# Memory keys and values projected two heads at a time, the filters' skip row added by a product with ones, and the decay gates' exponentials taken over four heads at once

## The chip, the cores and the metric

The kernel runs on one core of one Trainium2 chip. The metric is the device time of one execution in microseconds (us). A core has TensorE (PE in the rows, with its weight loads as PEld), VectorE (DVE), ScalarE (ACT), GpSimd (POOL) and SyncE (SP), whose queue issues the DMAs. Each engine works through its own list of instructions in order; an instruction that waits holds up everything behind it on its engine.

## What is computed

The reference is a trunk of two encoder layers on 512 tokens of width 1024, in fp32. Each layer runs three mixers side by side (attention with two key/value heads, a Hyena long convolution, gated linear attention), merges them with gates, then a cross-attention of four heads 256 wide into a memory of 256 tokens, then an MLP of width 4096. Three pieces of it matter here:

```
# cross-attention: keys and values of the memory, 4 heads of 256
k = rmsnorm((mn @ wk).reshape(B, M, X_HEADS, X_HEAD_DIM), kn)
v = (mn @ wv).reshape(B, M, X_HEADS, X_HEAD_DIM)
# Hyena: filters of order 2, normalised by their column sums of |f|, and a skip
f = f / (jnp.sum(jnp.abs(f), axis=0, keepdims=True) + EPS)
y = irfft(rfft(u, 2L) * rfft(f)) + u * skip
# gated linear attention: decay gates of 4 heads, two directions
g = jax.nn.log_sigmoid(lr @ w_lr + b_lr) / 16
b = jnp.cumsum(g, over a chunk of 64 tokens)      # then exp(b), exp(-b)
```

## The kernel before

Every fp32 product is made of three matmuls: `split` writes a rounded high part (a cast on ACT, `wh` or `xh`) and the rest (a subtraction on DVE, `wl` or `xl`), and `mm3` (L245 to L249) adds hi·hi, hi·lo and lo·hi into one PSUM tile. Weights come as chunks of 128 x 1024: a DMA into one of two `wr` buffers, a cast into one of three `wh`, a subtraction into one of three `wl`. A chunk of a token projection feeds 24 matmuls of 128x512.

The work of a layer is cut into generators (stages), and an order written out by hand (`ORDER0` for layer 0, `ORDER` for layer 1) says which stage emits its next piece. `kv` is the memory's keys and values, `mx` the norm of the layer's input, `gp` and `ga0` the linear attention's projections and gates, `fi` the Hyena filters, `at` the attention, `gh` the Hyena projection. A scheduler with priorities (`late`, `AHEAD`, `SPLIT_AHEAD`) makes each engine's list from that. The filters of layer 1 are made while PE runs the MLP of layer 0.

**Memory.** The stage works one head at a time, four values (V0 to V3), then four keys (K0 to K3). A head takes two chunks (4 k-tiles of 256 columns each), and its two token halves are two runs of `proj_tm` into one PSUM tile of 128 x 2 x 256: 24 matmuls of 128x256 for each half, 48 for a head and 384 for a layer. The stage keeps two PSUM tiles. A value is copied out by ACT. A key is squared by ACT (L1192), scaled by a reciprocal root of small DVE instructions (L347 to L352), multiplied by DVE (L1197), transposed and stored.

**Norm.** `mx` waits for a sum of squares `hsum` (L328), which PE adds over partitions (L336) and, after a reciprocal root, spreads over them (L358). DVE then multiplies eight tiles (`nrm`, L384) and makes their low parts (`xl`, L243), in part with POOL. The first product of the layer's input that follows is the gates' low-rank projection (L886, L888), which needs all eight `xl`.

**Filters.** A filter block (eight in all, four for each layer) has `acc`, the sums of absolute values by partition. PE adds them over partitions into a row of 1x256 with ones as the weights (L706, fp32), DVE multiplies the row by the skip weights on one partition (L712), and PE spreads the row over 128 partitions into the tile `T4[0]` with a row of ones (L718, fp32). A second product of `acc` (L708) gives the column sums as a column for the normaliser.

**Gates.** For each head PE makes the logits (L922), ACT takes Abs (L925), Exp (L928) and Ln (L933) in tiles of 128x512, POOL subtracts (L940), DVE scans forward and backward (L941, L943), POOL copies chunk ends (L955, L956), DVE shifts (L950), ACT takes the two exponentials (L952, L953), DVE multiplies queries and keys (L959, L960). Exp and Ln lie in different function tables of ACT, so a switch between them is an ACT_TABLE_LOAD. The gate `gt` of L1072 is a further exponential.

## Time and profile before

| | before |
|---|---|
| runs, us | 2300.2, 2301.21, 2303.95 (median 2301.21) |
| profiled execution, us | 2299.69 |
| its span from the first to the last instruction, us | 2297.8 |
| mean granted TensorE clock | 0.985 |
| PE busy | 2211.1 us, 96% of the span, 11432 instructions |
| DVE, ACT, POOL busy | 67%, 44%, 18% |

The profiled execution is 2299.69 us long; 1.9 us of it lie outside the span. Its busy time of PE counts an instruction from its start to its modelled end, and matmuls overlap, so what a matmul costs in a stream is read from start to start. A granted clock of 1.00 in a stretch means 2.4 GHz; half of it is 1.2 GHz.

### The profile page before, as it was taken

Reading aid. Unit: us, or ns where it says so; the run is one execution under the profiler, and the core shown is the slowest. Engines: PE = TensorE matmul, PEld = TensorE weight load, DVE = VectorE, ACT = ScalarE, POOL = GpSimd, SP = SyncE. Lnnn points to the kernel's source line nnn. Section 1 sums busy time; section 2 is a strip of 40 time slices with the busy share of each in tenths; the row PEclk is TensorE's granted clock in tenths of the full one; section 3 lists DMA queues with packets and bytes.
Section 4 is the critical chain, followed back from the end, with each engine's and each line's share of the span. In section 5 each row is a group of like instructions: output and inputs, shape, how many; then the busy total and the mean of one; then the engine's idle time right before and its main releaser. Section 6 shows DMA issues by size and latency. Waiting matters only on the chain.

```text
span 2297.8 us, 29857 instructions
## 1 busy us (share of the span) xinstructions
PE 2211.1 (96%) x11432; PEld 1857.2 (81%) x11432; DVE 1535.5 (67%) x2491; ACT 1013.0 (44%) x1635; POOL 418.1 (18%) x353
## 2 busy tenths in 40 slices
PE   6989999998899999999999989999989999999999
PEld 6877888887678878888887978888867788888887
DVE  7799856869665755766476786667886566444445
ACT  5667744323344544443336577443323444433231
POOL 1141101224220101111051130012253101000004
PEclk9999999999999999999999999999999999999999
DMA  6423123123143133332244321242222422323222
GB/s 224 146 97 106 65 74 123 56 93 101 60 149 113 63 122 103 122 122 101 92 143 143 105 79 41 74 128 65 83 101 74 141 89 74 101 92 101 94 94 97
DMA packets 78966, 232.58 MB, mean 101 GB/s; under 512 B 9054, under 2 KB 10086, under 8 KB 78824
## 3 DMA queue, kind: packets, MB, share of 16 engines
q1 hardware_dynamic: 75656, 224.91, 29.7%
q0 software_dynamic: 3168, 5.77, 0.9%
q8 instruction: 90, 1.47, 0.3%
q14 instruction: 52, 0.43, 0.1%
HBM read 213.87 MB, written 16.78 MB: 100 GB/s over the span
## 4 chain that ended last, share of the span: by engine, by line
PE 78%; DVE 13%; ACT 3%; DMA 2%; issue 2%; POOL 1%; SPq 0%; DVEq 0%; ACTq 0%; POOLq 0%
PE ps L249 24%; PE ps L247 24%; PE ps L248 24%; DVE wl L232 3%; PE ps L533 1%; ACT wh L231 1%; DVE ts L796 1%; PE ps L520 1%; PE ps L542 1%; PE ps L544 1%; DMA wr<-in_x_wv_dram 1%; PE ps L521 1%; DMA F<-F 1%; DVE u L797 1%; DVE ts L587 1%
## 5 line engine op out<-in xcount | busy, mean ns | idle before, releaser
L232 DVE TENSOR_TENSOR wl<-wr,wh 128x1024 fp32r<-128x1024 f32 x340 | 432.7, 1275 | 257.6 <-ACT wh L231 253.1
L231 ACT CAST wh<-wr 128x1024 fp32r<-128x1024 f32 x344 | 357.9, 1042 | 554.1 <-PE ps L248 459.8
L249 PE MATMUL ps<-xh,wl 128*128 128x512 f32 x1344 | 532.8, 397 | 17.2 <-DVE wl L232 17.2
L247 PE MATMUL ps<-xh,wh 128*128 128x512 f32 x1344 | 534.3, 398 | 2.3 <-ACT wh L231 2.0
L248 PE MATMUL ps<-xl,wh 128*128 128x512 f32 x1344 | 532.3, 396 | 0.0
L249 PEld LDWEIGHTS ps<-xh,wl 128*128 128x128 f32 x1344 | 255.4, 190 | 72.6 <-DVE wl L232 20.9
L247 PEld LDWEIGHTS ps<-xh,wh 128*128 128x128 f32 x1344 | 255.6, 190 | 55.7 <-ACT wh L231 3.3
L248 PEld LDWEIGHTS ps<-xl,wh 128*128 128x128 f32 x1344 | 255.6, 190 | 50.4
L249 PE MATMUL ps<-hdh,wl 128*128 128x512 f32 x512 | 199.9, 390 | 0.0
L247 PE MATMUL ps<-hdh,wh 128*128 128x512 f32 x512 | 199.7, 390 | 0.0
L248 PE MATMUL ps<-hdl,wh 128*128 128x512 f32 x512 | 199.2, 389 | 0.0
L1344 DVE TENSOR_TENSOR macc<-ps,macc 128x512 f32<-128x512 f32 x96 | 66.1, 689 | 86.0 <-PE ps L249 86.0
L249 PEld LDWEIGHTS ps<-hdh,wl 128*128 128x128 f32 x512 | 96.1, 188 | 22.1 <-issue 2.3
L248 PEld LDWEIGHTS ps<-hdl,wh 128*128 128x128 f32 x512 | 96.1, 188 | 19.9
L247 PEld LDWEIGHTS ps<-hdh,wh 128*128 128x128 f32 x512 | 96.1, 188 | 19.9 <-issue 0.3
L1346 POOL TENSOR_TENSOR macc<-macc,rb 128x512 f32<-128x512 f32 x16 | 23.6, 1472 | 398.4 <-DVE macc L1344 398.4
L248 PE MATMUL ps<-wl,xh 128*128 128x256 f32 x320 | 91.5, 286 | 0.8 <-DVE wl L232 0.8
L247 PE MATMUL ps<-wh,xh 128*128 128x256 f32 x320 | 91.4, 286 | 0.1
L249 PE MATMUL ps<-wh,xl 128*128 128x256 f32 x320 | 91.3, 285 | 0.0
L248 PE MATMUL ps<-wl,mnh 128*128 128x256 f32 x256 | 77.0, 301 | 13.9 <-DVE wl L232 13.8
L1328 DVE TENSOR_TENSOR rl<-rl 128x512 f32<-128x512 f32 x64 | 44.7, 699 | 65.9 <-ACT rl L1327 65.9
L247 PE MATMUL ps<-wh,mnh 128*128 128x256 f32 x256 | 76.2, 298 | 7.8 <-ACT wh L231 7.8
(404 smaller groups left out, 4570.8 us busy)
## 6 DMA issues: line engine op xcount, KB each, us to landing
wr<-in_mlp_w_dram SPq DMA_DIRECT2D x128, 512.0 KB, 3.5
wr<-in_w_in_dram SPq DMA_DIRECT2D x108, 512.0 KB, 3.6
wr<-in_x_wv_dram SPq DMA_DIRECT2D x16, 512.0 KB, 3.6
wr<-in_x_wk_dram SPq DMA_DIRECT2D x16, 512.0 KB, 4.0
F<-ff SPq DMA_DIRECT2D x32, 256.0 KB, 2.3
F<-F SPq DMA_DIRECT2D x32, 256.0 KB, 5.2
wr<-in_w_out_dram SPq DMA_DIRECT2D x16, 512.0 KB
wr<-in_x_wq_dram SPq DMA_DIRECT2D x16, 512.0 KB, 3.6
```

The lines of the kernel that those rows point to most:

```text
L231: r = self.nc.scalar.copy(hi, src)
L232: (lo_eng or self.nc.vector).tensor_tensor(lo, src, hi, op=ALU.subtract)
L247: mm(out, lh, rh, start=start, stop=False, skip_group_check=True)
L248: mm(out, lh, rl, start=False, stop=False, skip_group_check=True)
L249: mm(out, ll, rh, start=False, stop=stop, skip_group_check=True)
L520: nc.tensor.matmul(s, QH[:, tk], K2, start=True, stop=False)
L521: nc.tensor.matmul(s, QL[:, tk], K2, start=False, stop=True)
L533: nc.tensor.transpose(pt[:, k, i * P:(i + 1) * P], Pn[i][:, (2 * kp + k) * P:(2 * kp + k + 1) * P], self.ident)
L542: nc.tensor.matmul(ov, vv, TH[:, k], start=(kt == 0), stop=False, skip_group_check=True)
L1328: nc.vector.tensor_tensor(r, r, r, op=ALU.mult)
L1344: nc.vector.tensor_tensor(acc[m], ps, acc[m], op=ALU.add)
L1346: nc.gpsimd.tensor_tensor(acc[m], acc[m], rb, op=ALU.mult)
```

## The change

It has four parts.

Keys and values go two heads at a time (`proj_mem`): the weights are laid out on the host as chunks of 2 k-tiles of 512 columns, and each chunk is used for both token halves before the next. The moving operand is 512 wide, the two PSUM tiles hold one token half each, and a layer has 192 matmuls of 128x512 for 384 of 128x256. A pair has four copies or squares into the tiles of its two heads, and one reciprocal root for both keys.

The skip row is multiplied before it is summed: DVE multiplies all 128 partitions of `acc` (with EPS/128 added) by skip weights that the host has repeated on 128 partitions, splits the product, and two fp32r matmuls with a matrix of ones add it over partitions and spread it at once into `T4[0]`. The products L706 and L718 go, L708 (L741 after) stays. The ones are a tile of their own.

The four heads' gates share one tile `ab` of 128 x 4 x 512: four Abs, one Exp and one Ln over 2048 columns.

The order lists lose the `kv` pieces that are merged. K0 stood ahead of `mx` in both; now V01 and V23 stand ahead of it and K01 behind three pieces of `gp`.

```
-ORDER0: kv kv kv lx kv kv kv mx fi gp gp kv gp fi at at at gp at fi ... fi kv at kv ga0 at ...
+ORDER0: kv kv lx kv mx fi gp gp kv gp fi at at at gp at fi ... fi kv at ga0 at ...
-ORDER:  kv kv kv kv kv kv mx gp gp gp kv at at at at ga0 kv gp at ... gh gh gh kv gh ...
+ORDER:  kv kv kv mx gp gp gp kv at at at at ga0 gp at ... gh gh gh kv gh ...

+    def proj_mem(self, W, hp, X):
+        ps = [self.ps("mm") for _ in range(2)]
+        for g in range(4):
+            raw = self.wbuf("wr")
+            self.last_w = self.nc.sync.dma_start(raw, W[hp, g])
+            ...
+                self.split(raw, hi, lo)
+            for mt in range(2):
+                tk = slice(mt * P, (mt + 1) * P)
+                for k in range(2):
+                    kt = 2 * g + k
+                    self.mm3(ps[mt], X[kt][0][..., tk], X[kt][1][..., tk], hi[:, k], lo[:, k], kt == 0, kt == 7)
+        return ps

-                    nc.tensor.matmul(ps[0:1, 0:256], self.ones[:, 0:1], acc, start=True, stop=True)
...
-                row = self.rowbuf
-                self.load(row, I["hy_skip"][l, o, c])
-                nc.vector.scalar_tensor_tensor(row, ps[0:1, 0:256], EPS, row, op0=ALU.add, op1=ALU.mult)
-                with self.late("fr"):
-                    nc.tensor.matmul(T4[0][:, 0], self.ones[0:1, :], row, start=False, stop=True,
+                sa = self.t("F", (P, 2, 256), F32, "skip")[:, 0]
+                nc.vector.scalar_tensor_tensor(sa, acc, EPS / P, skip, op0=ALU.add, op1=ALU.mult)
+                sb = self.t("F", (P, 2, 256), F32R, "skip2")
+                self.split(sa, sb[:, 0], sb[:, 1])
+                with self.late("fr"):
+                    for x in range(2):
+                        nc.tensor.matmul(T4[0][:, 0], self.ones_r, sb[:, x], start=False, stop=(x == 1),

+        xs = self.t("ab4", (P, 4, L), F32, "ab")
         for h in range(4):
...
-            nc.scalar.activation(c, ps, AF.Abs, bias=b)
+            nc.scalar.activation(xs[:, h], ps, AF.Abs, bias=b)
...
-            nc.scalar.activation(c, c, AF.Exp, scale=-1.0)
-        for c in xs:
-            nc.scalar.activation(c, c, AF.Ln, bias=self.ones[:, 0:1])
+        nc.scalar.activation(xs, xs, AF.Exp, scale=-1.0)
+        yield
+        nc.scalar.activation(xs, xs, AF.Ln, bias=self.ones[:, 0:1])

-        for h in range(4):
-            w = self.wchunk(I["x_wk"][l], h)
+        for hp in range(2):
+            ps = self.proj_mem(I["x_wk"][l], hp, X)
...
-            self.rsqrt(rk, ss)
+            rk = self.tiny(4, "krs")
+            self.rsqrt(rk, ss)
```

Three places show how the instructions move. The line numbers of the changed kernel are its own.

PE at the start of layer 1, before: the last product of layer 0 (`hdh`), the sum of squares of the memory (L1160), the first matmuls of the memory's values (`mnh`, `mnl`), and, 120 of them later, the norm's sum over partitions (L336).

```order
L249 MATMUL ps_10226<-hdh_9945,wl_75 128x512
L1160 MATMUL ps_10287<-consts,memsq_10246 128x1 x4
L247 MATMUL ps_10312<-wh_71,mnh_10248 128x256
...
L248 MATMUL ps_10430<-wl_74,mnh_10281 128x256
L249 MATMUL ps_10430<-wh_70,mnl_10282 128x256
L336 MATMUL ps_10625<-consts,hsum_10107 128x1
L247 MATMUL ps_10430<-wh_72,mnh_10248 128x256
L336 MATMUL ps_10625<-consts,hsum_10107 128x1 x3
```

The same place in the changed kernel: L1184 is the memory's sum, L251 to L253 are `mm3`, L359 is the norm's sum and L381 its spread.

```order
L253 MATMUL ps_10028<-hdh_9747,wl_75 128x512
L1184 MATMUL ps_10089<-ones,memsq_10048 128x1 x4
L251 MATMUL ps_10108<-wh_72,mnh_10050 128x512
...
L253 MATMUL ps_10108<-wh_73,mnl_10062 128x512
L359 MATMUL ps_10248<-ones,hsum_9909 128x1 x4
L251 MATMUL ps_10108<-wh_73,mnh_10061 128x512
...
L253 MATMUL ps_10108<-wh_71,mnl_10073 128x512
L381 MATMUL ps_10265<-consts,small 128x128 x4
L251 MATMUL ps_10109<-wh_71,mnh_10072 128x512
```

The norm's sum stood behind 120 matmuls of the memory and now stands behind 15, with 81 of V01 and V23 behind it; K01 is no longer ahead of the norm at all.

ACT in the gates of layer 1, before: Exp (L928) and Ln (L933) of the third and fourth head, each with its table load, casts of weights (L231, `wh`) and the exponential of the gate (L1072, `gt`).

```order
L928 ACTIVATE ab_11605<-ab_11605 128x512
L925 ACTIVATE ab_11612<-ps_11610,consts 128x512
L933 ACT_TABLE_LOAD
L933 ACTIVATE ab_11605<-ab_11605,consts 128x512
L928 ACT_TABLE_LOAD
L928 ACTIVATE ab_11612<-ab_11612 128x512
L1072 ACTIVATE gt_11785<-ps_11760 128x512
L933 ACT_TABLE_LOAD
L933 ACTIVATE ab_11612<-ab_11612,consts 128x512
L231 CAST wh_72<-wr_69 128x1024
L952 ACT_TABLE_LOAD
L952 ACTIVATE mn_11593<-ab_11591 128x512
```

The same in the changed kernel, from the third head's Abs (L951) on: Exp is L955, Ln L957, the cast L235, the gate L1096.

```order
L951 ACTIVATE ab_11156<-ps_11167,consts 128x512
L951 ACTIVATE ab_11156<-ps_11172,consts 128x512
L955 ACTIVATE ab_11156<-ab_11156 128x2048
L1096 ACTIVATE gt_11346<-ps_11321 128x512
L957 ACT_TABLE_LOAD
L957 ACTIVATE ab_11156<-ab_11156,ones 128x2048
L235 CAST wh_71<-wr_70 128x1024
L235 CAST wh_72<-wr_69 128x1024
L1096 ACT_TABLE_LOAD
L1096 ACTIVATE gt_11373<-ps_11348 128x512
L976 ACTIVATE mn_11160<-ab_11156 128x512
```

All four heads' Ln stand in one instruction, and two casts of weights wait behind it.

DVE in the same gates, before: the scans (L941, L943), the reciprocal root of K2 (L350 to L352) and the two low parts of weights (L232) behind the fourth head's first scan.

```order
L941 SCALAR_TENSOR_TENSOR ab_11598<-reset_12221,mn_11600 64x512
L352 SCALAR_TENSOR_TENSOR small<-small 128x2
L950 TENSOR_TENSOR ab_11591<-ab_11591,small 128x512
L1197 SCALAR_TENSOR_TENSOR xk_11564<-ps_11515,small,xgain_10542 128x256 x2
L943 SCALAR_TENSOR_TENSOR ab_11598<-reset_12221,mn_11600 64x512
L941 SCALAR_TENSOR_TENSOR ab_11605<-reset_12221,mn_11607 64x512
L950 TENSOR_TENSOR ab_11598<-ab_11598,small 128x512
L943 SCALAR_TENSOR_TENSOR ab_11605<-reset_12221,mn_11607 64x512
L941 SCALAR_TENSOR_TENSOR ab_11612<-reset_12221,mn_11614 64x512
L232 TENSOR_TENSOR wl_74<-wr_69,wh_72 128x1024
L232 TENSOR_TENSOR wl_75<-wr_68,wh_70 128x1024
```

And after: L965 and L967 are the scans, L974 the shift, L236 the low parts of weights, L983 and L984 the products with queries and keys.

```order
L953 TENSOR_SCALAR mn_11175<-ps_11172,consts 128x512
L965 SCALAR_TENSOR_TENSOR ab_11156<-reset_11779,mn_11160 64x512
L236 TENSOR_TENSOR wl_76<-wr_70,wh_71 128x1024
L236 TENSOR_TENSOR wl_74<-wr_69,wh_72 128x1024
L967 SCALAR_TENSOR_TENSOR ab_11156<-reset_11779,mn_11160 64x512
L965 SCALAR_TENSOR_TENSOR ab_11156<-reset_11779,mn_11165 64x512
L974 TENSOR_TENSOR ab_11156<-ab_11156,small 128x512
L967 SCALAR_TENSOR_TENSOR ab_11156<-reset_11779,mn_11165 64x512
L965 SCALAR_TENSOR_TENSOR ab_11156<-reset_11779,mn_11170 64x512
L983 SCALAR_TENSOR_TENSOR qk_1677_10397<-qk_1677_10397,mn_11160 128x512
L984 TENSOR_TENSOR qk_1683_10465<-qk_1683_10465,ab_11156 128x512
```

The pair of low parts stood behind seven scans; now it stands behind the first alone, and the next one (`wl_75`) twelve instructions further on. The reciprocal root and the two products of K2 are gone from here.

## Rows read from the trace of the kernel before

**Rows 1.** The page: busy time, share of the span and instructions of each engine; the chain that ended last, by engine.
```profile
PE 2211.1 (96%) x11432; PEld 1857.2 (81%) x11432; DVE 1535.5 (67%) x2491; ACT 1013.0 (44%) x1635; POOL 418.1 (18%) x353
PE 78%; DVE 13%; ACT 3%; DMA 2%; issue 2%; POOL 1%; SPq 0%; DVEq 0%; ACTq 0%; POOLq 0%
```

**Rows 2.** The two longest sums in the waits of PE (waiting line, what it waited for: us in total, times, the longest).
```profile
PE ps L249 <- DVE wl L232: 31.4, 16, 5.2
PE ps L248 <- DVE wl L232: 14.6, 9, 5.9
```

**Rows 3.** Windows of 20 us: busy time and instructions of PE, PEld, DVE, ACT, POOL, then the granted clock of TensorE, the DMA share and GB/s.
```profile
40.00:60.00 20.00, 18.64 (x111) 15.85 (x112) 15.50 (x30) 9.48 (x18) 0.82 (x2) 0.85 0.63 190
140.00:160.00 20.00, 16.69 (x65) 12.94 (x66) 19.44 (x35) 16.04 (x22) 9.13 (x13) 0.74 0.26 80
1040.00:1060.00 20.00, 20.00 (x107) 17.15 (x106) 11.83 (x19) 10.43 (x16) 3.92 (x3) 1.00 0.16 54
1320.00:1340.00 20.00, 14.75 (x63) 11.84 (x63) 19.14 (x30) 14.85 (x24) 10.12 (x10) 0.90 0.21 69
```

**Rows 4.** The timeline of PE (start, duration, line, operation, tiles; idle time before and its releaser): nine steps of memory matmuls in a stream, then the wait of layer 0's start, and the first and last matmul at a low clock behind it (24 steps apart).
```profile
33.01 0.28 PE L247 MATMUL ps<-wh,mnh 128*128 128x256 f32 x1
34.09 0.28 PE L247 MATMUL ps<-wh,mnh 128*128 128x256 f32 x1
40.29 0.58 PE L248 MATMUL ps<-wl,mnh 128*128 128x256 f32 x1 [5.92 <-DVE wl L232]
40.67 0.41 PE L249 MATMUL ps<-wh,mnl 128*128 128x256 f32 x1
45.79 0.32 PE L249 MATMUL ps<-wh,mnl 128*128 128x256 f32 x1
```

**Rows 5.** The timeline of PE in the MLP of layer 0: two matmuls of 128x512 in a stream, 25 steps apart.
```profile
1100.13 0.39 PE L247 MATMUL ps<-xh,wh 128*128 128x512 f32 x1
1105.80 0.39 PE L248 MATMUL ps<-xl,wh 128*128 128x512 f32 x1
```

**Rows 6.** The timeline of PE in the MLP of layer 0, around the filter products of one block.
```profile
1061.78 0.39 PE L249 MATMUL ps<-xh,wl 128*128 128x512 f32 x1
1062.10 0.59 PE L706 MATMUL ps<-acc,consts 128*1 128x256 f32 x2
1062.62 0.61 PE L708 MATMUL ps<-consts,acc 128*128 128x1 f32 x4
1063.97 0.69 PE L718 MATMUL ps<-consts 1*128 1x256 f32 x2
1064.60 0.50 PE L247 MATMUL ps<-hdh,wh 128*128 128x512 f32 x1
```

**Rows 7.** The timelines of DVE, ACT and PE at the norm of layer 0: the first `nrm`, the wait of a cast for a key chunk, the low part that waited for the cast, the last `xl`, and the last instruction of the low-rank projection.
```profile
31.68 4.08 DVE L384 TENSOR_TENSOR nrm<-rb,h 128x512 f32<-128x512 f32 x3 [1.42 <-ACT rb L378]
47.71 1.05 ACT L231 CAST wh<-wr 128x1024 fp32r<-128x1024 f32 x1 [6.57 <-DMA wr<-in_x_wk_dram]
48.79 1.23 DVE L232 TENSOR_TENSOR wl<-wr,wh 128x1024 fp32r<-128x1024 f32 x1 [3.77 <-ACT wh L231]
51.73 0.74 DVE L243 SCALAR_TENSOR_TENSOR xl<-nrm,consts,xh 128x512 fp32r<-128x512 f32 x1
60.43 0.39 PE L888 MATMUL ps<-xl,wh 128*32 128x512 f32 x1
```

**Rows 8.** The timelines of PE and DVE at the start of layer 1: the sum of squares on DVE, the norm's sum on PE, PE's longest wait, the last `xl`, the low-rank projection's last instruction.
```profile
1198.48 0.68 DVE L328 TENSOR_TENSOR hsum<-hsum,hsq 128x512 f32<-128x512 f32 x1
1209.94 0.28 PE L336 MATMUL ps<-consts,hsum 128*128 128x1 f32 x2
1227.12 0.58 PE L248 MATMUL ps<-wl,mnh 128*128 128x256 f32 x1 [3.67 <-DVE wl L232]
1231.49 0.75 DVE L243 SCALAR_TENSOR_TENSOR xl<-nrm,consts,xh 128x512 fp32r<-128x512 f32 x1 [0.34 <-ACT xh L242]
1236.26 0.39 PE L888 MATMUL ps<-xl,wh 128*32 128x512 f32 x1
```

**Rows 9.** The timelines of ACT and PE in the gates of layer 0: a wait of ACT ahead of the first exponential with a cast behind it, and PE's wait for that cast.
```profile
142.38 0.63 ACT L952 ACTIVATE mn<-ab 128x512 f32<-128x512 f32 x1 [2.11 <-DVE ab L950]
142.92 1.03 ACT L231 CAST wh<-wr 128x1024 fp32r<-128x1024 f32 x1
144.00 0.80 PE L247 MATMUL ps<-xh,wh 128*128 128x512 f32 x1 [1.65 <-ACT wh L231]
```

**Rows 10.** The timelines of ACT, DVE and PE in the gates of layer 1: a table load and the Exp behind it, a scan, the pair of low parts of weights behind the scans, and the two waits of PE there.
```profile
1325.00 1.28 ACT L928 ACT_TABLE_LOAD   x1
1326.30 0.63 ACT L928 ACTIVATE ab<-ab 128x512 f32<-128x512 f32 x1
1332.16 1.22 DVE L941 TENSOR_TENSOR_SCAN ab<-reset,mn 64x512 f32<-64x512 f32 x1
1337.61 2.35 DVE L232 TENSOR_TENSOR wl<-wr,wh 128x1024 fp32r<-128x1024 f32 x2
1338.87 0.80 PE L249 MATMUL ps<-xh,wl 128*128 128x512 f32 x1 [5.25 <-DVE wl L232]
1352.04 0.30 PE L499 MATMUL ps<-consts,q 128*128 128x128 f32 x1 [1.43 <-ACT gt L1072]
```

**Rows 11.** The instructions on the tile `mn` (line, engine, operation, count: duration in ns, least, median and most; first and last start; forms): POOL's subtraction in the gates.
```profile
L940 POOL TENSOR_TENSOR mn<-mn,ab x8: 1257/1298/1890, 134.8 to 1334.1; 128x512 f32<-128x512 f32 x8
```

More of the change, by code (lines that the diff above doesn't have):

```diff
@@ L108, in laid_out @@
     o["w_glr"] = chunks(w[:, :, 3840:3872], 32)
[L109 to L110 removed]
+    for n in ("w_br_attn", "w_br_hyena", "w_br_gla", "w_out", "x_wq", "x_wo", "mlp_w1", "mlp_w2"):
         o[n] = chunks(a[n])
+    for n in ("x_wk", "x_wv"):
+        d, k, m = a[n].shape
+        o[n] = f(a[n].reshape(d, k // 256, 2, P, m // 512, 512).transpose(0, 4, 1, 3, 2, 5)).reshape(
+            d, m // 512, k // 256, P, 1024)
     col = lambda x: x.reshape(depth, -1, P).transpose(0, 2, 1)
@@ L289, in setup @@
         nc, cp = self.nc, self.cp
-        C = cp.tile([P, 1408], F32, name="consts")
-        self.rowbuf = C[0:1, 1152:1408]
+        C = cp.tile([P, 1280], F32, name="consts")
+        self.skip = C[:, 1024:1280]
+        self.ones_r = cp.tile([P, P], F32R, name="ones")
         self.small = cp.tile([P, 2 * SMALL], F32, name="small")
@@ L295, in setup @@
         self.turn = dict(wr=0, wh=0, wl=0)
-        self.ident, self.ones = C[:, 0:P], C[:, P:2 * P]
+        self.ident, self.ones = C[:, 0:P], self.ones_r.bitcast(F32)
         self.rope = C[:, 256:768].rearrange("p (a t d) -> p a t d", a=2, t=NT)
@@ L660, in filters @@
                 acc = self.t("s12", (P, 2, 256), F32, "acc")[:, 0]
+                skip = self.skip
+                self.load(skip, I["hy_skip"][l, o, c])
                 for par in (1, 0):
@@ L1183, in cross_kv @@
         G = G[:, 0]
-        for h in range(4):
-            w = self.wchunk(I["x_wk"][l], h)
-            ps = self.ps("mm", (P, 2, 256))
-            for mt in range(2):
-                self.proj_tm(ps[:, mt], w, slice(0, 256), X, slice(mt * P, (mt + 1) * P))
-            kk = self.t("st", (P, 2, 256), F32, "xk")
-            ss = self.tiny(2, "kss")
-            for mt in range(2):
-                nc.scalar.activation(kk[:, mt], ps[:, mt], AF.Square, accum_out=ss[:, mt:mt + 1])
-            nc.vector.scalar_tensor_tensor(ss, ss, 1.0 / 256, me, op0=ALU.mult, op1=ALU.add)
-            rk = self.tiny(2, "krs")
-            self.rsqrt(rk, ss)
-            for mt in range(2):
-                nc.vector.scalar_tensor_tensor(kk[:, mt], ps[:, mt], rk[:, mt:mt + 1], G,
-                                               op0=ALU.mult, op1=ALU.mult)
-            pt = self.ps("b", (P, 2, 256))
-            for dt in range(2):
-                for mt in range(2):
-                    with self.late("kt"):
-                        nc.tensor.transpose(pt[:, dt, mt * P:(mt + 1) * P],
-                                            kk[:, mt, dt * P:(dt + 1) * P], self.ident)
-            xk = self.t("xk", (P, 2, 256), F32, "xk")
-            nc.scalar.copy(xk, pt)
-            nc.sync.dma_start(self.kvd[h].rearrange("p (a b) -> p a b", a=2), xk)
@@ new lines, in cross_kv @@
+        for hp in range(2):
+            ps = self.proj_mem(I["x_wk"][l], hp, X)
+            kks = []
+            ss = self.tiny(4, "kss")
+            for j in range(2):
+                kk = self.t("st", (P, 2, 256), F32, "xk")
+                for mt in range(2):
+                    nc.scalar.activation(kk[:, mt], ps[mt][:, 256 * j:256 * j + 256], AF.Square,
+                                         accum_out=ss[:, 2 * j + mt:2 * j + mt + 1])
+                kks.append(kk)
+            for j in range(2):
+                s2 = ss[:, 2 * j:2 * j + 2]
+                nc.vector.scalar_tensor_tensor(s2, s2, 1.0 / 256, me, op0=ALU.mult, op1=ALU.add)
+            rk = self.tiny(4, "krs")
+            self.rsqrt(rk, ss)
+            for j in range(2):
+                kk = kks[j]
+                for mt in range(2):
+                    nc.vector.scalar_tensor_tensor(kk[:, mt], ps[mt][:, 256 * j:256 * j + 256],
+                                                   rk[:, 2 * j + mt:2 * j + mt + 1], G, op0=ALU.mult, op1=ALU.mult)
+            for j in range(2):
+                kk = kks[j]
+                pt = self.ps("b", (P, 2, 256))
+                for dt in range(2):
+                    for mt in range(2):
+                        with self.late("kt"):
+                            nc.tensor.transpose(pt[:, dt, mt * P:(mt + 1) * P],
+                                                kk[:, mt, dt * P:(dt + 1) * P], self.ident)
+                xk = self.t("xk", (P, 2, 256), F32, "xk")
+                nc.scalar.copy(xk, pt)
+                nc.sync.dma_start(self.kvd[2 * hp + j].rearrange("p (a b) -> p a b", a=2), xk)
```

51 lines of the change are left out of this document (24 added, 27 removed).

## The prediction

> **What bounds the kernel now.** The page comes first: PE is busy 96% of the span and the chain that ended last runs 78% through PE [rows 1]. So time is won in two ways only: less work on PE, or less of its waiting. The waits of PE come next: nearly all are for low parts of weights, 46 us in 25 waits [rows 2]; a low part is a DVE instruction, so these are places where DVE is late. The windows show where [rows 3]: at 40 to 60, 140 to 160 and 1320 to 1340 us PE loses both busy time and clock (0.85, 0.74, 0.90), with DVE at 19.1 to 19.4 of 20 in the last two; in the MLP (1040 to 1060) PE is 20.00 of 20 at a clock of 1.00. There every PE step removed is time won; near the two starts and the gates a step removed may only lengthen a wait.
>
> The timeline gives the price of a step, from start to start. Memory matmuls of 128x256: 1.08 us for nine steps, 0.120 each; at the low clock 5.12 us for 24, 0.213 each [rows 4]. Matmuls of 128x512: 5.67 us for 25, 0.227 each [rows 5].
>
> **The change, part by part.** All gains are in us of PE's end.
>
> *Filters in the MLP: +4.0.* Around L706, 0.84 us pass from one `mm3` step to the next product; a plain step is 0.227, so L706's pair costs 0.61. L718's pair takes 0.63 to the next step [rows 6]. Removed 1.24 a block, added two 256-wide fp32r steps at 0.12, net 1.0; four blocks lie here. If the new pair breaks the stream as L706 did, 0.63 a block remains: 2.5. The DVE, ACT work added (a multiplication, a cast, a subtraction of 128x256) lies beside a PE that waits for neither here. Bounds 2.5 to 5.
>
> *Filters of layer 0: +2.0.* The same 4.0, but in a stretch where DVE is as full as PE [rows 3]. Each block has one more DVE instruction (the subtraction) there. I take half; bounds 0 and 4.
>
> *Memory matmuls.* A head costs 48 x 0.120 = 5.76 before and 24 x 0.227 = 5.44 after, so 0.32 a head and 5.1 for all 16. The lower bound is 0 (two half-wide steps as dear as a wide one). The values are inside the two start terms below; the keys of layer 1 stand in stretches bound by PE: +1.3; those of layer 0 in the DVE-bound stretch, half: +0.7.
>
> The Trainium skill (TensorE: Matmul & The Clock Gate, "Wait — 56ns, not 53.3ns?") gives a warm matmul N/2.4 GHz plus about 2.5 ns, which is an estimated 109 and 216 ns here and 0.06 us a head, 1.0 in all. The rows, 120 and 227, differ from it; by the page the whole forecast would be about 1.7 us longer, 2284.
>
> *Start of layer 0: +3.0.* DVE goes from the first `nrm` at 31.68 to the last `xl`, ending at 52.47, in 20.8 us, 3.77 of them idle for the cast of a key chunk, which waited 6.57 for its DMA [rows 7]. K0's chunks are no longer ahead, so that wait goes and the last `xl` ends near 48.7. The low-rank projection is 16 steps of 0.23; it ended at 60.8, now at 48.7 + 3.7 = 52.4: 8.4 earlier. K0's 5.44 is still to be done later, so 3.0 is won. The wait of 5.92 for a low part behind three `nrm` [rows 4] stays in some form: the `nrm` are still ahead of it in DVE's list. If taking K0 out of the gap only lengthens PE's idling, the gain is 0; if K0 later fills a wait, 6.
>
> *Start of layer 1: +4.0.* DVE had the sum of squares at 1199.16, PE added it at 1209.94 only, since 120 memory matmuls stood ahead [rows 8]. With 15 ahead it runs at about 1199.2, 10.7 earlier. If the chain to the last `xl` (end 1232.24) moves with it, that ends at 1221.5, the projection at 1225.3 instead of 1236.65: 11.3 earlier, 5.9 after K0's 5.44 is paid. Off that, two things. V23's first matmul needs a PSUM tile that V01 held (both tiles are one pair's; before, heads alternated): three copies of 256 columns, each about 0.3 to 0.4 by the 1.03 of a 1024-column cast [rows 9], an estimated 1.0. And V23's four low parts fall between the `nrm`, with DVE and POOL both at work: 0.9. The 3.67 wait for a low part [rows 8] does not vanish: PE has 81 matmuls (18.4 us) to cover 22 us of the norm. Bounds 0 and 6.
>
> *Gates of layer 1: +2.6.* Before: waits of 5.25 and 1.43 [rows 10]. After, the first scan needs all four heads. From the second pair of logits: Abs twice 1.3; Exp of 2048 columns; `gt` 0.6; load 1.28; Ln; POOL's subtraction 1.30 [rows 11]; scan 1.22. Exp of 512 is 0.63 [rows 10], a 1024 cast 1.03 [rows 9], so 0.40 per 512 and 1.83 for 2048. Sum 9.4, then a low part of 1.23 [rows 7]: 10.6. Two chunks have their low parts ahead of it in DVE's list, 48 x 0.227 = 10.9 of PE: a wait of 0 to 1.4, say 0.7. The next low part but one stands behind six scans (7.3) and six 128x512 instructions at the 0.75 of an `xl` [rows 8] (4.5); with two low parts that is 14.3 against 10.9 of PE: a wait of 3.4. So 4.1 for 6.7. What leaves this queue is the reciprocal root and products of K2; K2's 5.8 us of matmuls, which covered PE here, leave too, and that is in the count of chunks. Bounds -8 (PE has no chunk ahead) and +8.7 (no wait, and the 2.0 us that a clock of 0.90 costs in 20).
>
> *Gates of layer 0: +1.0.* Now a cast stands behind an exponential that waited 2.11 for DVE, PE waits 1.65 for that cast [rows 9], and the clock of 0.74 costs 5.2 in the window [rows 3]. The four loads fewer per layer are 5.1 us of ACT, but two casts now stand behind load and Ln, 3.1 in a piece. Bounds -8 and +6.9.
>
> Two reciprocal roots fewer in a layer take DVE time off; I count it in the terms above. DMAs keep their number; the eight skip loads carry 128 KB for one row and are needed long after issue.
>
> Sum: 4.0 + 2.0 + 1.3 + 0.7 + 3.0 + 4.0 + 2.6 + 1.0 = 18.6. The profiled execution took 2299.7, of which the span is 2297.8; so 2281.1. It lies 1.5 under the median of the runs, 2301.2, so I forecast 2282 to 2283 and write 2282.
>
> **The rivals.** 0.2% is 4.6 us, about what a measurement of this kernel can tell from no change.
>
> (a) *The gates in one piece starve PE in both layers; slower.* For it: the first scan is one DVE instruction with two low parts queued behind it, and the chain to it is serial. If PE has no chunk ahead, the first wait is 10.6; if the scans also wait for POOL's four subtractions (5.2), the second is 8.6; 24 steps at the low clock lose 2.2. That is 21.4 a layer, 42.8, against 15.6 now (5.25 + 1.43 + 2.0, and 1.65 + 5.2). It costs 27 where the other terms give 15: 2313. It decides from 35 us of such loss, 17.6 a layer. Against it: the casts and low parts of two chunks are ahead in the lists.
>
> (b) *Only arithmetic pays.* At both starts PE idles through the norm as DVE dictates, and removing K0 buys nothing. 4.0 + 2.0 + 5.1 = 11: 2290. For it: DVE at those places makes what PE waits for.
>
> (c) *The waits go too.* ACT and DVE lose loads and reciprocal roots just where they are late; the gates' 15.6, starts of 6 and 6, all 8 of the filters and 2.5 of the keys: 38, so 2263.
>
> (d) *No change.* As (a), but without POOL's part: 16.2 a layer, 32.4 against 15.6, so 17 lost for 15 won: 2303.
>
> (e) *A wide step wins next to nothing over two narrow ones.* If the step is N columns and a small fixed cost, the memory matmuls give 1.7 less and 2284 comes out; the rows at 0.120 and 0.227 speak against it. The page cited above states this rule.
>
> **How the numbers follow.** The forecast as summed (2273 to 2288) 0.53; (e), inside it, 0.05; (b) 0.15; (c) 0.12; (d) 0.08; (a) 0.07. The predicted time is that of the first. Leaving out (a) and (d) leaves 0.85, and the range runs from (c)'s 2264 to 2297, past (b)'s 2290 by the 7 us that the gates can add to it. Faster by over 0.2% holds all but (d) and (a), 0.85; within, 0.08; slower, 0.07.
>
> **What will show it.** In the profile after: memory matmuls of 128x512 at 0.227 a step, 384 of them; in the MLP, a filter block with two steps of 0.12 where 1.24 stood, and PE still 20.00 of 20; the norm's sum on PE within a microsecond of DVE's at layer 1's start, and the low-rank projection's end about 11 before its place then, with one key head more behind it; at layer 0's start no wait of a cast for a key chunk and that projection done near 52; in layer 1's gates a wait under 1.5 before the first low part behind a scan and one of about 3.4 after it. I am wrong if PE idles over 10 us in a gate stage, if PE's gap at the starts grows by what K0 filled, or if the fp32r pair costs as much as the two fp32 products. A wait of PE for a copy of V01 above 1 us would be the PSUM tile mis-sized.

## The result and the profile after

The changed kernel takes 2287.8 us (median of 4 runs, 2285.6 to 2291.0), the kernel before beside it 2300.7: 0.9944 of it, interval 0.9932 to 0.9957. Timed again later beside three experiments it gave 0.9945 (0.9933 to 0.9958). So 13 us are won where 18.6 were forecast: the direction and the range held, and the gain came out a third smaller.

The page after: busy time of each engine, and the chain by engine. They answer to [rows 1].

```profile
PE 2196.0 (96%) x11032; PEld 1827.7 (80%) x11032; DVE 1530.7 (67%) x2455; ACT 1001.3 (44%) x1623; POOL 416.8 (18%) x353
PE 71%; DVE 11%; issue 2%; DMA 2%; ACT 2%; POOL 0%; SPq 0%; DVEq 0%; ACTq 0%; POOLq 0%
```

PE's share is as before: its busy time fell from 2211.1 to 2196.0 us, and the rest of the span did not fall (86.7 before, 88.5 after). Its longest sums of waits after (answer to [rows 2]):

```profile
PE ps L253 <- DVE wl L236: 32.3, 18, 4.6
PE ps L251 <- ACT wh L235: 14.7, 11, 7.5
PE ps L252 <- DVE wl L236: 9.3, 7, 2.8
PE ps L543 <- ACT qh L531: 3.8, 1, 3.8
```

Before, the waits for casts of weights and for `qh` were these:

```profile
PE ps L247 <- ACT wh L231: 12.1, 8, 7.6
PE ps L520 <- ACT qh L508: 0.5, 2, 0.2
```

Low parts still cost 41.6 us in 25 waits for 46.0 in 25, casts of weights cost 14.7 for 12.1, and the wait for `qh` rose from 0.5 to 3.8.

To see where the 13 us lie, the program is cut at PE instructions that both kernels have. The table gives the us that each stretch takes in a profiled execution (the changed kernel twice). Up to some cuts (the ends of A, H, I and J) the changed kernel has one key head still to do that the kernel before has done; "net" is before less after with that head set at 5.44 us.

| stretch, up to | before | after | again | net gain | forecast |
|---|---|---|---|---|---|
| A: layer 0's low-rank projection | 60.4 | 52.7 | 53.2 | +2.3, +1.8 | +3.0 |
| B: the first logits | 66.4 | 69.7 | 70.6 | +2.1, +1.2 | 0 |
| C: the linear attention's norm (337 us) | 210.2 | 211.2 | 213.0 | -1.0, -2.8 | +3.7 |
| D: the cross-attention's norm (692 us) | 355.0 | 357.1 | 357.3 | -2.1, -2.3 | 0 |
| E, F: the first filter block in the MLP | 188.8 | 187.2 | 187.2 | +1.6, +1.6 | 0 |
| G: the end of the MLP | 314.0 | 308.8 | 308.8 | +5.2, +5.2 | +4.0 |
| H: layer 1's low-rank projection | 41.6 | 31.4 | 31.2 | +4.8, +5.0 | +4.0 |
| I: layer 1's last logits | 82.6 | 82.0 | 82.2 | +0.6, +0.4 | +1.3 |
| J: the attention's scores behind the gates | 58.1 | 58.5 | 58.5 | -0.4, -0.4 | +2.6 |
| K: the last norm | 575.5 | 580.6 | 580.3 | +0.3, +0.6 | 0 |

The sums are 13.4 and 10.3, as the profiled executions have it (2299.69 against 2286.31 and 2289.47).

How much a stretch varies from one execution to the next can be read too. The changed kernel was profiled twice, and two experiments change only layer 1; up to the end of G all four have the same instructions in the same order on PE, DVE, ACT and POOL. They took 121.6 to 126.1 us for A + B, 211.2 to 213.7 for C, 356.5 to 357.3 for D, 187.2 to 190.4 for E + F, and 308.8 each time for G. So one execution shows a difference of 5 us or less in A + B, and of 2 to 3 in C or E + F, no better than as a hint. The kernel before has one profiled execution.

The rows that answer to the groups of before follow.

A filter block in the MLP, PE's timeline after (answer to [rows 6]): L741 is the column sum, L735 the skip product.

```profile
1055.28 0.39 PE L253 MATMUL ps<-xh,wl 128*128 128x512 f32 x1
1055.50 0.28 PE L741 MATMUL ps<-ones,acc 128*128 128x1 f32 x2
1055.64 0.36 PE L735 MATMUL ps<-skip,ones 128*128 128x256 f32 x1
1055.84 0.28 PE L741 MATMUL ps<-ones,acc 128*128 128x1 f32 x2
1055.98 0.36 PE L735 MATMUL ps<-skip,ones 128*128 128x256 f32 x1
1056.18 0.39 PE L251 MATMUL ps<-hdh,wh 128*128 128x512 f32 x1
```

The pair takes 0.20 a step, a little more than the 0.12 counted (in the three other blocks, where it stands between steps of `mm3`, 0.12); from the last step of one `mm3` to the next, 0.90 us pass. Before, that stretch is in two pieces, 1.31 (1061.78 [rows 6] to 1063.09) and 0.96 (1063.64 to 1064.60 [rows 6]), with one step of `mm3` at the start of each:

```profile
1063.09 0.49 PE L247 MATMUL ps<-hdh,wh 128*128 128x512 f32 x1
1063.41 0.40 PE L248 MATMUL ps<-hdl,wh 128*128 128x512 f32 x1
1063.64 0.40 PE L249 MATMUL ps<-hdh,wl 128*128 128x512 f32 x1
1064.94 0.40 PE L248 MATMUL ps<-hdl,wh 128*128 128x512 f32 x1
```

The starts, PE's timeline after (answer to [rows 4], [rows 7] and [rows 8]): the wait at layer 0's norm and the end of its low-rank projection, the norm's sum of layer 1, the longest wait there, and that projection's end.

```profile
39.02 0.67 PE L252 MATMUL ps<-wl,mnh 128*128 128x512 f32 x1 [2.84 <-DVE wl L236]
52.74 0.39 PE L914 MATMUL ps<-xl,wh 128*32 128x512 f32 x1
1191.29 1.05 PE L359 MATMUL ps<-ones,hsum 128*128 128x1 f32 x8
1203.56 0.50 PE L252 MATMUL ps<-wl,mnh 128*128 128x512 f32 x1 [1.34 <-DVE wl L236]
1218.14 0.40 PE L914 MATMUL ps<-xl,wh 128*32 128x512 f32 x1
```

The projection of layer 0 ends 7.7 earlier, that of layer 1 18.1 earlier of which 7.9 were won before the layer began. No wait for a copy of V01 shows at V23's first matmul.

Layer 1's gates after, timelines of ACT, POOL, DVE and PE in the order of time (answer to [rows 10] and [rows 11]): Ln in one piece, three of POOL's subtractions, the first scan, the pair of low parts, PE's four waits, and what the last of them hangs on.

```profile
1308.21 2.01 ACT L957 ACTIVATE ab<-ab,ones 128x2048 f32<-128x2048 f32 x1
1310.29 4.78 POOL L964 TENSOR_TENSOR mn<-mn,ab 128x512 f32<-128x512 f32 x3 [16.29 <-ACT ab L957]
1311.63 2.30 DVE L965 TENSOR_TENSOR_SCAN ab<-reset,mn 64x512 f32<-64x512 f32 x1 [7.06 <-POOL mn L964]
1313.85 4.67 DVE L236 TENSOR_TENSOR wl<-wr,wh 128x1024 fp32r<-128x1024 f32 x2
1316.20 0.50 PE L253 MATMUL ps<-xh,wl 128*128 128x512 f32 x1 [1.38 <-DVE wl L236]
1327.34 3.56 POOL L981 TENSOR_TENSOR small<-small 128x4 f32<-128x4 f32 x1
1328.33 0.50 PE L251 MATMUL ps<-xh,wh 128*128 128x512 f32 x1 [0.95 <-ACT wh L235]
1330.89 0.50 PE L253 MATMUL ps<-xh,wl 128*128 128x512 f32 x1 [1.83 <-DVE wl L236]
1332.30 0.69 DVE L974 TENSOR_TENSOR ab<-ab,small 128x512 f32<-128x512 f32 x1 [1.47 <-POOL small L973]
1335.90 1.22 PE L543 MATMUL ps<-k,qh 128*128 128x512 f32 x2 [3.81 <-ACT qh L531]
```

Four waits sum to 8.0 us, for 6.7 before. Three of POOL's subtractions run in a row behind the one Ln, the fourth soon after, and beside them the scan takes 2.30 us for 1.22 and each of two low parts 2.33 for 1.23.

### The profile page after: what moved, and what is told of

It reads as the page before. It is cut to its first block, busy times and chain, and to the rows that moved or that the text cites. A ratio compares the mean times of both kernels' runs of the same rounds, so it can differ in the third digit from the quotient of the medians.

```text
span 2284.5 us, 28960 instructions
## 1 busy us (share of the span) xinstructions
PE 2196.0 (96%) x11032; PEld 1827.7 (80%) x11032; DVE 1530.7 (67%) x2455; ACT 1001.3 (44%) x1623; POOL 416.8 (18%) x353
## 3 DMA queue, kind: packets, MB, share of 16 engines
q1 hardware_dynamic: 76792, 225.95, 31.4%
## 4 chain that ended last, share of the span: by engine, by line
PE 71%; DVE 11%; issue 2%; DMA 2%; ACT 2%; POOL 0%; SPq 0%; DVEq 0%; ACTq 0%; POOLq 0%
PE ps L253 22%; PE ps L251 22%; PE ps L252 22%; DVE wl L236 3%; DVE ts L822 1%; DMA F<-F 1%; PE ps L556 1%; ACT wh L235 1%; DVE u L823 1%; DVE held L823 0%; PE ps L1311 0%; DVE ts L610 0%; PE ps L543 0%; PE ps L544 0%; PE ps L565 0%
## 5 line engine op out<-in xcount | busy, mean ns | idle before, releaser
L236 DVE TENSOR_TENSOR wl<-wr,wh 128x1024 fp32r<-128x1024 f32 x340 | 437.3, 1289 | 245.2 <-ACT wh L235 240.8
L235 ACT CAST wh<-wr 128x1024 fp32r<-128x1024 f32 (+1 forms) x344 | 357.7, 1042 | 513.2 <-PE ps L252 422.7
L253 PE MATMUL ps<-xh,wl 128*128 128x512 f32 x1344 | 530.3, 395 | 17.7 <-DVE wl L236 17.7
L251 PE MATMUL ps<-xh,wh 128*128 128x512 f32 x1344 | 531.7, 396 | 4.8 <-ACT wh L235 4.4
L253 PEld LDWEIGHTS ps<-xh,wl 128*128 128x128 f32 x1344 | 253.9, 189 | 73.8 <-DVE wl L236 22.9
L251 PEld LDWEIGHTS ps<-xh,wh 128*128 128x128 f32 x1344 | 254.4, 189 | 59.4 <-ACT wh L235 6.8
L253 PE MATMUL ps<-hdh,wl 128*128 128x512 f32 x512 | 199.4, 390 | 0.0
L251 PE MATMUL ps<-hdh,wh 128*128 128x512 f32 x512 | 199.2, 389 | 0.0
L253 PEld LDWEIGHTS ps<-hdh,wl 128*128 128x128 f32 x512 | 96.1, 188 | 19.9
L251 PEld LDWEIGHTS ps<-hdh,wh 128*128 128x128 f32 x512 | 96.1, 188 | 19.8
L251 PE MATMUL ps<-wh,xh 128*128 128x256 f32 x320 | 91.7, 287 | 0.0
L253 PE MATMUL ps<-wh,xl 128*128 128x256 f32 x320 | 91.2, 285 | 0.0
L351 POOL TENSOR_TENSOR hsum<-hsum,hsq 128x512 f32<-128x512 f32 x30 | 43.4, 1445 | 166.8 <-ACT hsq L349 166.8
L1356 ACT ACTIVATE rl<-ps 128x512 f32<-128x512 f32 x64 | 37.9, 591 | 77.9 <-PE ps L253 77.9
```

Of the source, the lines that this page charges most:

```text
L235: r = self.nc.scalar.copy(hi, src)
L236: (lo_eng or self.nc.vector).tensor_tensor(lo, src, hi, op=ALU.subtract)
L251: mm(out, lh, rh, start=start, stop=False, skip_group_check=True)
L253: mm(out, ll, rh, start=False, stop=stop, skip_group_check=True)
L351: eng.tensor_tensor(self.hsum, self.hsum, sq, op=ALU.add)
L1356: nc.scalar.activation(r, ps, AF.Relu)
```

## The experiments

Ratios are to the kernel before on the same chip, with intervals; 0.001 is 2.3 us.

| kernel | ratio |
|---|---|
| skip alone | 0.9994 (0.9986 to 1.0003) |
| gates alone | 0.9999 (0.9990 to 1.0007) |
| wide keys and values alone | 0.9995 (0.9985 to 1.0005) |
| narrow heads at the new places | 1.0072 (1.0057 to 1.0087) |
| wide, gates | 0.9991 (0.9980 to 1.0001) |
| wide, skip | 0.9952 (0.9941 to 0.9964) |
| skip, gates | 0.9992 (0.9983 to 1.0000) |
| wide, skip in layer 0's blocks alone | 0.9964 (0.9951 to 0.9976) |
| all three, keys moved forward in layer 1 | 0.9940 (0.9927 to 0.9953) |
| all three, again | 0.9945 (0.9933 to 0.9958) |
| all three, gates head by head in layer 1 | 0.9946 (0.9932 to 0.9960) |
| all three, first keys ahead of the norm | 0.9976 (0.9967 to 0.9985) |

**One part at a time.** Each kernel is the kernel before with one part of the diff above (the gates with the one line that gives `ab4` its buffer, the wide keys with their order lists).

> The kernel before with the filters' skip as a product with ones and nothing else. Theory A (a PE step saved counts only where PE is full): the four blocks in the MLP of layer 0 give about 6.6 us, as in the changed kernel, the four of layer 0 give 0 to 1 because VectorE sets the pace there; time near 2294 (2292 to 2296). Rival B (every block counts alike, and the changed kernel lost its gain of layer 0 to another part): about 13 us, near 2288.

> The kernel before with one Exp and one Ln over four heads and nothing else; the keys of the third head still stand in layer 1's gates. Theory G (one piece bunches POOL's subtractions and the scans, and this ate the gain in layer 1's gates): slower than before by 2 to 6 us, 2303 to 2307, with PE waits in layer 1's gate stage above the 6.7 us of before. Rival C (the one piece is good by its fewer table loads, and the loss in the changed kernel is that the third head's matmuls no longer cover the stage): faster by 1 to 4, 2297 to 2300, with PE waits there below 6.7.

> The kernel before with keys and values two heads wide in the changed kernel's order lists; filters and gates as before. Theory A: about 2 us at layer 0's start, 5 at layer 1's, 1 from the keys of layer 1: 2292 to 2294. Theory G adds: layer 1's gate stage has waits of at most 6.7 us. Rival C: without the third head's matmuls as cover its waits are above 6.7 and the time is 2295 to 2299.

None of the three is told from no change, and most of the expected times failed: the skip (2300.1) and the wide keys (2299.8) lie outside both of their ranges. The gates (2299.4) lie inside rival C's. The stretches of the table say why this is not the same as "does nothing":

| us | before | skip | gates | wide |
|---|---|---|---|---|
| A + B | 126.8 | 124.4 | 128.9 | 124.2 |
| C | 210.2 | 214.0 | 208.5 | 217.0 |
| D | 355.0 | 355.3 | 355.2 | 359.5 |
| G | 314.0 | 308.7 | 313.9 | 314.0 |
| H | 41.6 | 41.8 | 42.9 | 30.2 |

The skip gives its 5.3 in the MLP, and nothing else gives or takes anything there; the wide keys give their 11.4 (6.0 net) in H. Theory A held in these places. The 2 us or so of A + B lie within the spread of executions. But the skip lost 3.8 in C, and the wide keys 6.8 in C and 4.5 in D, where A had expected 0 to 1. PE's timeline of the kernel with the skip alone shows its loss in C in one wait of the logits for a VectorE instruction:

```profile
143.99 1.19 PE L926 MATMUL ps<-lr,wlr 96*128 96x512 f32 x2 [6.88 <-DVE rv L426]
```

Before, the wait of the logits was 2.01 there. For the gates, J took 59.5 for 58.1 and PE's waits in it sum to 7.1 us for 6.7, so C (better by its loads) fails although the time lies in its range; G has the sign of the stage right, and its 2 to 6 us did not come as a whole.

**The places without the width.**

```
-ORDER0: kv kv kv lx kv kv kv mx fi gp gp kv gp ... fi kv at kv ga0
+ORDER0: kv kv kv lx kv kv mx fi gp gp kv kv gp ... fi kv kv at ga0
-ORDER:  kv kv kv kv kv kv mx gp gp gp kv at at at at ga0 kv gp ... gh gh gh kv gh
+ORDER:  kv kv kv kv kv mx gp gp gp kv kv at at at at ga0 gp ... gh gh gh kv kv gh
```

> The kernel before with its narrow heads, one after the other, at the places that the pairs have in the changed order lists; nothing else. If what the memory part gains is its places (the norm's sum earlier, the first key behind the norm): 2294 to 2297, 2 to 4 us behind the wide pairs, which save 0.32 us a head. If it is the width (fewer, wider matmuls and one reciprocal root for two heads): within 2 us of the kernel before.

Both expectations fall: it is slower by 16.6 us. H is 34.0, for 35.8 before without K0's 5.76 and 30.2 with wide pairs alone, so the start gains a little by the place, and at layer 0's norm PE's wait stays at 5.92, where wide pairs alone have 2.82; B, C and K (77.2, 220.3, 590.6 for 71.4, 217.0, 580.3 with wide pairs, the same heads in each) lose more. The places pay with the pairs alone.

**Two parts at a time.** Each is the changed kernel with one part of the diff taken back.

> The changed kernel with the old skip (keys and values wide, gates in one piece). Theory I (the wide keys lose in layer 0's gate stage, where table loads and exponentials head by head hold back the casts of weights, PE waits 3.82 and 3.36 there with wide keys alone; one Exp and one Ln take this away): 2291 to 2295, about 7 to 8 faster than wide keys alone, with no wait above 2.5 in layer 0's gates and the MLP of layer 0 as before. Rival S (the parts only shift each other's order by chance, and the gain of 13 needs all three): 2296 to 2301.

> The changed kernel with Exp and Ln head by head (keys and values wide, skip by ones). Theory I: only the MLP's filters are won over wide keys alone, about 5, so 2293 to 2296, and the wait of layer 0's gate stage (3.82 and 3.36) is still there. Theory G of before (the one piece costs PE's waits in layer 1's gates, 1.38, 0.95, 1.83 and 3.81 in the changed kernel): 2284 to 2287, faster than the changed kernel.

> The changed kernel with narrow keys and values in the old order lists (skip by ones, gates in one piece). Theory I: 5 to 6 from the MLP and little else, 2293 to 2297. Rival S: within 3 of the kernel before, as the two parts alone.

Wide keys and skip together give 11 us where each gave 1; neither other pair is told from no change. Theory I (the gates' one piece rescues the wide keys) falls with the first of these: 2300.5, not 2291 to 2295, and a wait of 3.50 in layer 0's gates where none above 2.5 was expected. It falls with the third too, 1.8 us for 5 to 6. Theory S falls with the second: two parts give most of the 13. The second, at 2291.2, lies between its two ranges, so theory G's 2284 to 2287 fails for the whole: without the one piece J is 55.6 for 58.5, but the time is not below the changed kernel's.

**Where wide keys and skip meet.** The kernel with wide keys and skip, with the old row in the MLP's blocks:

```
+                if l == 0:
+                    sa = self.t("F", (P, 2, 256), F32, "skip")[:, 0]
...
+                else:
+                    ps = self.ps("b", (P, L))
+                    row = skip[0:1]
...
```

> Keys and values two heads wide, Exp and Ln head by head, and the skip by ones in the four filter blocks of layer 0 alone; those in the MLP have the old row. Theory I2 (what wide keys and the skip give together beyond their single gains lies in layer 0's stretch, where VectorE no longer waits for PE's row in front of its queue): about 6 of the 11 us, 2294 to 2297. Rival M (it lies in the MLP, where four blocks give all of it): 2298 to 2301, as with wide keys alone.

0.9964 is 8.3 us, 7 of them beyond wide keys alone: I2's place holds (2292.9, a microsecond under its range), and rival M falls. In the stretches, C goes from 217.0 to 210.8 by the skip in layer 0, though the same skip beside narrow keys lengthened it from 210.2 to 214.0. The mechanism that I2 named is not borne out: in the traces of the kernel before and of the wide keys alone, VectorE waits for PE's row in C for no more than 1.0 us together. What the traces show is in the windows of C, for the kernel before, the skip alone, the wide keys alone, and both (this kernel). The first two figures behind the window are its length and PE's busy time; the clock is the third figure from the end.

```profile
126.81:336.99 210.18, 199.22 (x1213) 169.67 (x1212) 173.47 (x311) 144.71 (x274) 46.19 (x56) 0.98 0.27 89
124.41:338.42 214.01, 198.01 (x1208) 170.47 (x1207) 175.57 (x319) 143.50 (x275) 46.81 (x56) 0.97 0.28 91
124.19:341.18 216.99, 201.22 (x1165) 167.72 (x1164) 171.26 (x300) 145.14 (x274) 48.55 (x55) 0.97 0.28 87
121.42:332.23 210.81, 195.74 (x1159) 165.97 (x1158) 173.32 (x308) 143.09 (x275) 57.14 (x56) 0.98 0.29 93
```

PE is idle for 11.0 us in C before, for 16.0 with the skip, for 15.8 with the wide keys, and for 15.1 with both (14.2 in the kernel with wide keys and skip, which has the same instructions there). So beside narrow keys the skip saves 1.2 us of PE's busy time and loses 5.0 to waits. Beside wide keys, which have brought as much waiting already, it brings no more, and of the 6.2 us won there 5.5 are PE's busy time: the products of three filter blocks, and a clock of 0.98 for 0.97. Each figure is that of one execution, and why the waits do not add up stays open.

**The cover of layer 1's gates.**

```
-ORDER: ... ga0 gp at at at ga0 ... gh gh gh kv gh
+ORDER: ... ga0 kv gp at at at ga0 ... gh gh gh gh
```

> The changed kernel with the second pair of keys of layer 1 moved forward to the place where the third head stood before (two pieces of the gates' stage earlier in the order list). Theory C (the gate stage of layer 1 gained nothing because the third head's matmuls no longer cover it): its waits fall from 8.0 us (1.38, 0.95, 1.83, 3.81) to under 4 and the time is 2283 to 2285. Rival (VectorE and POOL set the pace there whatever PE has to do, and the pair adds a reciprocal root and four products to VectorE's list): 2287 to 2291.

Theory C falls. PE's waits in the stage are the same four, to 0.06 us, with the keys' matmuls ahead of them:

```profile
1332.20 0.50 PE L253 MATMUL ps<-xh,wl 128*128 128x512 f32 x1 [1.44 <-DVE wl L236]
1344.34 0.50 PE L251 MATMUL ps<-xh,wh 128*128 128x512 f32 x1 [0.95 <-ACT wh L235]
1346.90 0.50 PE L253 MATMUL ps<-xh,wl 128*128 128x512 f32 x1 [1.83 <-DVE wl L236]
1351.92 1.22 PE L543 MATMUL ps<-k,qh 128*128 128x512 f32 x2 [3.79 <-ACT qh L531]
```

The time is that of the changed kernel, 0.9940.

**Head by head in layer 1, and the changed kernel beside it.**

```
+            if l == 1:
+                nc.scalar.activation(xs[:, h], xs[:, h], AF.Exp, scale=-1.0)
...
+        for x in ([xs] if l == 0 else [xs[:, h] for h in range(4)]):
+            nc.scalar.activation(x, x, AF.Ln, bias=self.ones[:, 0:1])
```

> The changed kernel as it is, timed beside the next three on one chip. Every theory: 0.993 to 0.996 of the kernel before.

> The changed kernel with the one piece of Exp and Ln kept in layer 0 and taken head by head in layer 1. Theory H (the one piece relieves ScalarE where layer 0's filters crowd it, and costs in layer 1's gates, where four subtractions on POOL then run beside the scans and two low parts at twice their time): 2 to 4 us faster than the changed kernel beside it, waits in layer 1's gate stage under 6 for its 8.0. Rival (the stage costs the same either way, and the difference between the ledgers is the spread of single executions): within 1.5 us of the changed kernel.

In the stage H is right: one wait is left, and J is 54.8 for 58.5. The four kernels with wide keys and gates head by head have a J of 54.8 to 56.0; the changed kernel, the one without the skip, the one with keys moved forward and the one with the first keys ahead of the norm have 58.5 to 59.8. The one piece costs some 3.5 us there.

```profile
1323.96 0.50 PE L253 MATMUL ps<-xh,wl 128*128 128x512 f32 x1 [4.25 <-DVE wl L236]
```

But the whole is 0.9946 for 0.9945: the rival's number, with intervals of 3 us to either side. In the profiled execution 3.2 of the 3.7 are paid back at the start of the MLP's filters (F), 54.8 for 51.6. A wait of 2.04 us for ACT stands there in both; the windows of the changed kernel, then of this one, then of the kernel before (2.19) show what follows it. The clock is the third figure from the end.

```profile
840.00:860.00 20.00, 20.00 (x89) 16.53 (x89) 13.41 (x19) 10.16 (x15) 0.00 (x0) 1.00 0.35 107
840.00:860.00 20.00, 20.00 (x74) 15.24 (x73) 13.55 (x19) 9.81 (x14) 0.00 (x0) 0.84 0.23 69
840.00:860.00 20.00, 20.00 (x79) 15.74 (x80) 14.53 (x20) 10.33 (x16) 0.00 (x0) 0.91 0.24 79
```

PE did 89 matmuls, 74 and 79. This loss can't be the doing of the edit: up to the end of G the two kernels have the same instructions in the same order. Eight profiled executions have this wait of 2.04; in four the clock stayed (the changed kernel twice, with keys moved, without the skip) and E + F took 187.0 to 187.2, in four it fell to 1.2 GHz (this one, the wide keys alone, without the one piece, with the first keys ahead) and E + F took 188.5 to 190.5. From the end of G on, where the two kernels differ, the profiled executions have 1095.1 us for 1097.8 and 1097.6. So the gain in the stage is shown, and that the whole time keeps it is not.

**The keys ahead of the norm.**

```
-ORDER0: kv kv lx kv mx fi gp gp kv gp     +ORDER0: kv kv lx kv kv mx fi gp gp gp
-ORDER:  kv kv kv mx gp gp gp kv at        +ORDER:  kv kv kv kv mx gp gp gp at
```

> The changed kernel with the first pair of keys back ahead of the norm in both order lists. Theory P (the starts gain because the keys are behind the norm): the low-rank projections end 6 to 10 later in both layers, the time is 3 to 7 above the changed kernel beside it. Rival E (the norm's sum stays early in PE's list and is what counts; the keys would fill PE while VectorE makes the norm): within 2 us of it, or faster.

In the changed kernel the pair stands behind two pieces of `gp` in layer 0 and behind three in layer 1. With it ahead of the norm the kernel is about 7 us slower than the changed kernel beside it (0.9976 for 0.9945): by the time, theory P, at its upper end. Its other sign missed: the low-rank projections end 12.8 and 13.2 later in their stretches, not 6 to 10, and 10.9 of that are the matmuls of the pair itself. Cut where both have done the same work, layer 0 takes 127.3 (A + B) for the 121.6 to 126.1 of the four executions above, and layer 1 takes 113.9 from the end of G to the third of its four logits, for 113.4, 113.4 and 114.1. So the traces show 1 to 6 us in layer 0 and no loss in layer 1, and where the rest of the 7 lies stays open. Rival E is not tested cleanly: with the pair ahead, layer 1's norm sum stands behind 41 matmuls of the memory for 15, and comes 10.2 us into the layer for 4.6.

## Why the prediction was right in its direction and too large

**The MLP's filters, +4.0: right, a little small.** G gives 5.2 in every kernel with the new skip there (308.7 to 308.8) and nothing in those without (313.9 to 314.5). The 0.3 a block that was left out is the neighbours: beside the fp32 products three more steps of `mm3` took 0.32 (1063.09 to 1063.41), 0.33 (1063.64 to 1063.97) and 0.34 us (1064.60 to 1064.94), for 0.227. The 1.6 of E + F was in no term and is luck as far as the traces go: it hangs on the clock after one wait, which differs between executions of the same instructions.

**The starts, +3.0 and +4.0: right in size.** A is 2.3 and 1.8, H 4.8 and 5.0. The wait of 5.92 is 2.84 after, by the width and not the place, since narrow heads at the new places still have 5.92. The term of 1.0 for V01's tile was not there. Of each, 1.6 is the arithmetic of five heads at 0.32, so rival (b), that only arithmetic pays, falls in H; in A the rest is within the spread of executions. By the time alone, 2287.8, (b)'s 2290 was nearer than 2282. That K0 behind the norm was the point is shown in part only: the last experiment lost 7 us in the whole, but none of it in layer 1 up to the logits.

**Layer 0's filters, keys and gates, +3.7: wrong, by the traces in sign too.** C gave -1.0 and -2.8. The work did become less there: PE's busy time in C fell from 199.2 us to 196.5 and 197.0. But PE's idle time in C, which the sum had a microsecond lower in the gates, rose from 11.0 to 14.7 and 16.1. The kernel before has one profiled execution, so the sign is a hint; that the 3.7 did not come is clear of the spread. I halved arithmetic for a VectorE that is full [rows 3]; there the gain is not a half, since PE's steps are not what ends last. I looked for the cost of the pair of keys in arithmetic alone and missed its low parts. Before, the two heads lay 34 us apart from first to last and PE waited for none of their low parts; as a pair they take 20 us, at four chunks with one low part each, in VectorE's fullest stretch. PE's timeline after:

```profile
152.65 0.50 PE L252 MATMUL ps<-wl,mnh 128*128 128x512 f32 x1 [1.55 <-DVE wl L236]
159.82 0.49 PE L251 MATMUL ps<-wh,mnh 128*128 128x512 f32 x1 [0.77 <-ACT wh L235]
161.94 0.70 PE L252 MATMUL ps<-wl,mnh 128*128 128x512 f32 x1 [1.62 <-DVE wl L236]
```

These are 3.9 us, two of the waits for low parts and one for a cast, and as much as the idle time rose. That they are the cause is not shown: other waits came and went, and with the gates head by head the pair waits 1.2 us while PE is still idle 14.2 to 15.1 us in C. The window at 140 that had lost clock has it back in part (0.74 before, [rows 3]):

```profile
140.00:160.00 20.00, 17.69 (x74) 13.93 (x72) 18.22 (x29) 9.56 (x10) 10.46 (x11) 0.96 0.32 98
```

**Layer 1's gates, +2.6: wrong, -0.4.** The prediction had waits of 0.7 and 3.4. The first came as 1.38, the second as 0.95 and 1.83; what failed is that the sum stopped there. Durations were taken as they are alone, and beside POOL's subtractions a scan and two low parts took twice as long (rows above). And nothing was counted for what is queued behind the heads' exponentials on ACT: `qh` waited for them, they for VectorE's shifts, and these for POOL's small instructions, one of 3.56 us. That gave 3.81. The wider piece is the cause, not the cover that K2 gave: the experiments with keys moved forward and with gates head by head tell these apart. With the gates head by head the four kernels with wide keys have a J of 54.8 to 56.0 for 58.1 before, about the gain that was forecast for the one piece.

**Layer 0 from 337 to 692 us, forecast untouched: -2.1 and -2.3.** All instructions stand in the old order, but four loads of filter spectra land later. SP's queue, before and then after (from the first issue to the last landing), and PE's wait behind them after, 4.43 for 3.03:

```profile
532.44 5.78 SPq L258 DMA_DIRECT2D F<-F  x4
529.36 7.23 SPq L262 DMA_DIRECT2D F<-F  x4
543.30 0.80 PE L251 MATMUL ps<-zh,dft 128*128 128x256 f32 x2 [4.43 <-ACT zh L235]
```

Bytes in flight are alike (3.71 and 3.75 MB from 500 to 560 us). In the traces, these loads take 6.6 to 7.2 with wide keys, 5.8 with narrow ones, and 6.3 with narrow ones at the new places; why is open. Nor is it shown that they are all of the loss: with wide keys and the skip in layer 0 alone they took 6.6, PE's wait was 3.03, and D was still 356.1.

**The keys' arithmetic.** Steps of 128x512 took 0.227 to 0.228 in V01 after, so a head did cost 5.44, and stretch I, with two heads of layer 1 in either kernel, gave 0.6, as two times 0.32 would. Rival (e) isn't told from it by the time, but is by these steps. Rival (c) falls with the waits that stayed. Rivals (a) and (d) fall with the time; of (a), the price in J came in part (3.5 us against head by head), far from its point of decision.

One reading ahead of the sum was wrong too: "nearly all" of PE's waits were said to be for low parts, but the 46.0 us are little more than half of the 86.7 in which PE was not busy, and casts of weights were 12.1 of the rest.

The forecast added eight gains as if each stood alone. The parts measured alone add up to 2.8 us at most by their ratios, 0.0006 + 0.0001 + 0.0005, and together they give 13. That no single part would be seen was in no rival.
